# Gate inputs of the later groups as eight fp32 products in four column groups, placed between two groups; two steps of the sample tile moved by thirds of a block

## The chip, the cores and the metric

One NeuronCore of a Trainium2 chip runs the whole program. TensorE (PE, with its weight loads on PEld), VectorE (DVE), ScalarE (ACT), GpSimd (POOL) and the queue engine SyncE (SP) work side by side and wait for one another by semaphores. The metric is the device time of one execution in microseconds. Times below are medians of several executions, or, where a trace is read, those of one profiled execution.

## The reference, cut to what matters

One layer of a hybrid encoder trunk: 2048 prompt frames (16 tiles of 128 rows) and 8 running streams of 16 frames (one tile, number 16, called the sample tile).

```python
h = rmsnorm(x, norm_mix_pre)
P = h @ w_in                       # q|k|v (3*512) | z (512) | b (4) | a (4) | B | C | H
q, k, v = conv4 + SiLU, l2norm(q), l2norm(k)
beta = sigmoid(b_raw)              # one per row and head
g = -exp(a_log) * softplus(a_raw + dt_bias)
S_t = exp(g_t) (I - beta_t k_t k_t^T) S_{t-1} + beta_t k_t v_t^T      # chunked, 4 heads x 128 x 128
o = rmsnorm(S_t^T q_t) * SiLU(z)
x = x + rmsnorm(concat(o, B * conv3(C * H)) @ w_o)
x = x + rmsnorm((silu(h2 @ w_gate) * (h2 @ w_up)) @ w_down)
```

The change is in the gates `b` and `a`, which are eight columns of `w_in`, and in the recurrence of the sample tile, whose eight streams have a state of their own for each head.

## The kernel before

**Stages.** The first third of the time (to about 870 us of the trace) is the projection and the recurrence; then come the output projection, the feed-forward network and its down projection. The change is in the first stage alone.

**Groups and blocks.** The 17 row tiles are worked in five groups (`GROUPS`) of 4, 4, 3, 3 and 3 tiles; the sample tile is the last of group 3 (groups are counted from 0). For a group, `w_in` goes through PE as 28 blocks of 128 columns (`SEQS`). Each block is an fp32 product made of three fp32r products (high by high, high by low, low by high) for each of the eight slices `k` of the 1024 inputs: 24 matmuls at L317, with 512 or 384 moving columns. A block is issued in three thirds (slices 0 to 2, 3 to 5, 6 and 7); after each third the program runs the steps that stand in `events` for that moment. The moments of a group are numbered 0 to 83, three to a block, and what is due at 84 or later falls into the next group.

**What sets the order.** PE's order is written out by hand (`manual_schedule`); it is the order in which `plan` puts the steps, by the table `PLAN` and the constants in `plan`. The order of ACT, DVE, POOL and SP is made by a scheduler from priorities and a timing model. Every engine, and the SP queue, takes its instructions strictly in order.

**Rows of the next group.** While a group runs, the columns `xT` of the next one are loaded (`x_load`, L268), scaled in place by the rows' factors (`x_norm`, L274, DVE) and split into `hi` and `lo` (`split`, L231 on ACT and L232 on DVE) with the gain of the norm. The `hi` and `lo` pools have `KD + NHX` = 10 buffers, so two slices (`NHX`) are split ahead, and `next_rows` splits the other six at the group's end, as the last block frees the buffers. Loaded slices lie in a ring of `XKB` = 4 buffers, the last two in another.

**Gates.** `wba` holds the eight gate columns as high part (8) and rest (8). `gate_matmuls` (L469) multiplies them with `hi` and `lo` of all eight slices: 16 fp32r matmuls with 16 output rows. In groups 1 to 4 this is done at moment 2, after the first block. `gate_products` scales the result (L480, ACT), and `gate_rates` turns each tile (L487, from 16 rows to 128 x 16), adds the two halves on DVE (L493, L494) and goes on to the rates.

**Sample tile.** Its recurrence is spread over the end of group 3 and the start of group 4, head by head, 7 moments apart. For head h with u = 65 + 7h: load the states (u - 2 or u - 4), spread k and q over column groups on POOL (u), the products with the states (u + 3; L794, four column groups of 32, fp32), the solve (u + 5; L800), the output (u + 7; L804), and at u + 10 the update of the states: four products (L812) into four banks and eight DVE instructions (L814) that add them to the states. Then `out_norm` at u + 10 and `out_turn` (L708) at u + 15 of the last head.

**Banks.** PSUM's eight banks are shared: three `dbank` for blocks, two `tbank` for turning, two `gbank` and one `obank`. The update of a head takes both `gbank`, the `obank` and one `tbank`; the next user of each waits until DVE has read it. The chunks of the prompt tiles use the same banks: L727 and L743 (`gbank`), L735 (`obank`), then L749 (`gbank`), whose result DVE adds to the state at L752, and L757 (`obank`), read at L758; L708 (`tbank`), read at L710.

Of the kernel before, what the change touches and what calls it, by code (L numbers as in the profile page):

```python
# [17 lines left out]
P = 128  # L18
# [35 lines left out]
XKB = 4  # L54
NHX = 2
# [35 lines left out]
def kernel(  # L91
# [66 lines left out]
    with ExitStack() as ph:  # L158
# [313 lines left out]
        def gate_products(g, ps=None):  # L472
            n, c = g["n"], g["n"] * P
            ps = ps or gate_matmuls(g["hi"], g["lo"], n)
            bsb = xbuf()[:16]
            src = ps[:16, :c]
            if g["rb"] is not None:
                src = bsb[:, :c]
                V.tensor_mul(src, ps[:16, :c], g["rb"][:16, :c])
            A.activation(bsb[:, :c], src, AF.Identity, scale=gsct[:, 0:1], bias=gbia[:, 0:1])  # L480
            g["bsb"] = bsb

        def gate_rates(g):
            n, bsb = g["n"], g["bsb"]
            ps = bank()
            for i in range(n):
                T.transpose(ps[:, i * 16:(i + 1) * 16], bsb[:, i * P:(i + 1) * P], ident[:16, :16])  # L487
# [3 lines left out]
            ps3 = ps[:, :16 * n].rearrange("p (t c) -> p t c", c=16)  # L491
            y3 = yv[:, :m].rearrange("p (t c) -> p t c", c=8)
            V.tensor_copy(y3, ps3[:, :, 0:8])  # L493
            V.tensor_add(y3, y3, ps3[:, :, 8:16])  # L494
# [333 lines left out]
        def plan(g, nx, events):  # L828
# [8 lines left out]
            if gi:  # L837
                at(2, gate_products, g)
# [114 lines left out]
        gsct, gbia = vec[:16, 145:146], vec[:16, 146:147]  # L953
# [7 lines left out]
        wba = gp.tile([P, KD, 16], F32R, name="wba")  # L961
# [17 lines left out]
        rb2 = small.tile([P, W1], F32, tag="rb2", name="rb2", bufs=1)  # L979
# [13 lines left out]
        for gi, tiles in enumerate(GROUPS):  # L993
# [3 lines left out]
            if gi == 0:  # L997
                g["rb2"] = rb2
            nx = {} if gi + 1 < len(GROUPS) else None
# [643 lines left out]
def pack(i):  # L1643
# [22 lines left out]
    gates[:16, 4] = ([-1.0] * 4 + [1.0] * 4) * 2  # L1666
# [41 lines left out]
```

## Time and profile before

| | |
|---|---|
| median of 3 runs | 2463.88 us (2463.84 to 2475.24) |
| profiled execution | 2467.25 us, its span 2465.5 us |
| granted PE clock, mean of the span | 0.997 |
| PE busy | 2434.2 us, 99% of the span |
| DVE, ACT, POOL busy | 66%, 42%, 23% of the span |
| L317, the blocks of the first stage | 3360 matmuls |
| L469, the gates' products | 80 matmuls, 16 in each group |

The page gives busy times, the chain that ended last and groups of instructions. A row of the timeline gives the start in us, the length in us, the engine, the line, the operation with the tiles it writes and reads, and in brackets the idle time of the engine just before it and who ended that. A matmul on PE is longer than its share of the engine, since matmuls are pipelined: what one costs is read from one start to the next. An fp32 matmul appears as two instructions, an fp32r one as one.

### The profile page before, as it was taken

Reading aid. Unit: us, or ns where it says so; the run is one execution under the profiler, and the core shown is the slowest. Engines: PE = TensorE matmul, PEld = TensorE weight load, DVE = VectorE, ACT = ScalarE, POOL = GpSimd, SP = SyncE. Lnnn points to the kernel's source line nnn. Section 1 sums busy time; section 2 is a strip of 40 time slices with the busy share of each in tenths; the row PEclk is TensorE's granted clock in tenths of the full one; section 3 lists DMA queues with packets and bytes.
Section 4 is the critical chain, followed back from the end, with each engine's and each line's share of the span. In section 5 each row is a group of like instructions: output and inputs, shape, how many; then the busy total and the mean of one; then the engine's idle time right before and its main releaser. Section 6 shows DMA issues by size and latency. Waiting matters only on the chain.

```text
span 2465.5 us, 39355 instructions
## 1 busy us (share of the span) xinstructions
PE 2434.2 (99%) x14376; PEld 2227.0 (90%) x14376; DVE 1619.8 (66%) x3082; ACT 1045.3 (42%) x2338; POOL 578.9 (23%) x663
## 2 busy tenths in 40 slices
PE   9999999999999999999999999999999999999997
PEld 7888889999989988899999999999999988887886
DVE  6875755755666466888788744456456565677698
ACT  6545545546444343444343422234333345333343
POOL 1101001001110000146565300000000046455563
PEclk9999999999999999999999999999999999999999
DMA  7774655666776566598877788878988743333466
GB/s 273 262 243 155 223 194 195 248 225 225 261 257 226 182 204 226 188 335 298 293 267 258 279 258 269 256 241 275 305 295 284 249 147 117 115 113 124 131 222 192
DMA packets 263465, 561.38 MB, mean 228 GB/s; under 512 B 25188, under 2 KB 144680, under 8 KB 245992
## 3 DMA queue, kind: packets, MB, share of 16 engines
q1 hardware_dynamic: 146864, 486.98, 57.5%
q10 hardware_dynamic: 116184, 70.85, 9.5%
q8 instruction: 113, 1.85, 0.3%
q0 software_dynamic: 224, 1.05, 0.1%
q14 instruction: 80, 0.66, 0.1%
HBM read 400.09 MB, written 158.70 MB: 227 GB/s over the span
## 4 chain that ended last, share of the span: by engine, by line
PE 88%; DVE 5%; DMA 2%; issue 2%; POOL 2%; ACT 1%; SPq 0%; DVEq 0%; ACTq 0%; POOLq 0%
PE fbank L1335 35%; PE dbank L317 26%; PE fbank L1512 11%; PE dbank L1100 4%; PE tbank L1100 4%; DVE xr L1535 1%; PE tbank L375 1%; POOL dw L1185 1%; DVE acc L1472 1%; PE gbank L469 1%; PE gbank L580 1%; PE gbank L587 1%; PE obank L735 1%; PE gbank L727 1%; POOL as L1495 1%
## 5 line engine op out<-in xcount | busy, mean ns | idle before, releaser
L1335 PE MATMUL fbank<-xh,fw 128*128 128x384 f32 (+1 forms) x3696 | 897.7, 326 | 2.5 <-ACT m L1369 2.3
L317 PE MATMUL dbank<-hi,w 128*128 128x384 f32 (+1 forms) x2240 | 655.1, 363 | 1.3 <-ACT w L296 0.7
L1335 PEld LDWEIGHTS fbank<-xh,fw 128*128 128x128 f32 x3696 | 651.1, 188 | 3.7 <-ACT m L1369 2.6
L1335 PE MATMUL fbank<-xl,fw 128*128 128x384 f32 (+1 forms) x1848 | 601.8, 326 | 0.0
L317 PEld LDWEIGHTS dbank<-hi,w 128*128 128x128 f32 x2240 | 413.6, 188 | 39.4 <-DVE w L297 1.3
L1512 PE MATMUL fbank<-dw,as 128*128 128x512 f32 x1782 | 420.1, 392 | 3.0 <-DVE as L1495 0.9
L1512 PEld LDWEIGHTS fbank<-dw,as 128*128 128x128 f32 x1782 | 332.9, 188 | 81.7 <-POOL as L1495 3.5
L317 PE MATMUL dbank<-lo,w 128*128 128x384 f32 (+1 forms) x1120 | 400.5, 358 | 0.5 <-DVE lo L232 0.5
L1335 PEld LDWEIGHTS fbank<-xl,fw 128*128 128x128 f32 x1848 | 346.9, 188 | 0.0
L317 PEld LDWEIGHTS dbank<-lo,w 128*128 128x128 f32 x1120 | 211.2, 189 | 16.8 <-DVE lo L232 0.8
L1495 POOL TENSOR_TENSOR as<-ar,as 128x256 fp32r<-128x256 f32 (+1 forms) x202 | 184.5, 925 | 170.7 <-ACT as L1492 162.9
L1472 DVE TENSOR_TENSOR acc<-acc,fbank 128x512 f32<-128x512 f32 x248 | 164.9, 681 | 90.1 <-PE fbank L1512 77.0
L1185 POOL TENSOR_TENSOR dw<-dr,dw 128x512 fp32r<-128x512 f32 x48 | 70.5, 1481 | 496.3 <-ACT dw L1183 496.2
L1492 ACT CAST as<-ar 128x256 fp32r<-128x256 f32 (+1 forms) x287 | 116.4, 427 | 166.5 <-PE fbank L1512 128.8
L1310 ACT CAST fw<-rg 128x512 fp32r<-128x512 f32 x124 | 77.2, 622 | 229.9 <-PE fbank L1335 132.6
L321 DVE SCALAR_TENSOR_TENSOR acc<-R,vec,acc 128x512 f32<-128x512 f32 (+2 forms) x180 | 120.9, 672 | 33.2 <-ACT acc L358 28.2
L1383 DVE TENSOR_TENSOR c<-u,fbank 128x384 f32<-128x384 f32 (+1 forms) x66 | 34.8, 528 | 96.5 <-PE fbank L1335 96.5
L1379 DVE TENSOR_TENSOR m<-m,m 128x384 f32<-128x384 f32 (+1 forms) x44 | 23.1, 525 | 83.0 <-ACT m L1369 82.9
L1311 POOL TENSOR_TENSOR fw<-rg,fw 128x512 fp32r<-128x512 f32 x44 | 65.3, 1484 | 44.6 <-ACT fw L1310 44.3
L1386 ACT ACTIVATE c<-c 128x384 f32<-128x384 f32 (+1 forms) x66 | 33.4, 506 | 93.6 <-DVE c L1385 93.6
L350 POOL COPY hist<-R 128x3 f32<-128x3 f32 x60 | 20.3, 338 | 220.8 <-ACT R L326 171.4
L1381 ACT ACTIVATE m<-fbank 128x384 f32<-128x384 f32 (+1 forms) x66 | 31.2, 473 | 92.2 <-PE fbank L1335 76.6
(386 smaller groups left out, 3590.7 us busy)
## 6 DMA issues: line engine op xcount, KB each, us to landing
w<-wsplit SPq DMA_DIRECT2D x105, 1024.0 KB, 4.9
fw<-fsplit SPq DMA_DIRECT2D x188, 512.0 KB, 4.7
fsplit<-fw SPq DMA_DIRECT2D x94, 512.0 KB, 3.7
partd<-pt ACTq DMA_DIRECT2D x86, 384.0 KB, 6.2
rg<-in_w_gu SPq DMA_DIRECT2D x62, 512.0 KB, 4.2
wsplit<-w SPq DMA_DIRECT2D x28, 1024.0 KB, 4.8
wr<-in_w_in SPq DMA_DIRECT2D x34, 512.0 KB, 5.9
ar<-partd SPq DMA_DIRECT2D x43, 384.0 KB, 3.1
```

The costliest lines, as they stand in the source:

```text
L317: T.matmul(ps[:, :c], l[:, k, :], r[k][:, :c], start=(k == 0 and r is hi and l is wh), stop=(k == KD - 1 and l is wl))
L321: r = V.scalar_tensor_tensor(acc, raw(d), w[:, d:d + 1], acc, op0=ALU.mult, op1=ALU.add)
L1100: T.matmul(pss[n], m_[:, j, :], w_[k][:, n * 512:(n + 1) * 512], start=(k == 0 and ci == 0), stop=(k == KD - 1 and ci == 2))
L1185: e.tensor_tensor(out=w[1], in0=v, in1=w[0].bitcast(F32), op=ALU.subtract)
L1310: A.copy(w[:, 0], v)
L1311: e.tensor_tensor(out=w[:, 1], in0=v, in1=w[:, 0].bitcast(F32), op=ALU.subtract)
L1335: T.matmul(ps, w_[:, c], b_[k][:, :hw], start=(first and k == 0 and ci == 0), stop=(k == KH - 1 and ci == 2), skip_group_check=not first)
L1383: V.tensor_add(c21, u2, b3)
L1472: return eng.tensor_tensor(out=dst, in0=dst, in1=ps, op=ALU.add)
L1492: ins = A.copy(a[:, 0, :n], v)
L1495: e.tensor_tensor(out=a[:, 1, :n], in0=v, in1=a[:, 0, :n].bitcast(F32), op=ALU.subtract)
L1512: T.matmul(ps, a[:, x_, q * P:(q + 1) * P], w[y_], start=(start and q == 0 and ci == 0), stop=(q == c - 1 and ci == 2), skip_group_check=True)
```

## The change

Gates of groups 1 to 4. A new function `gate_parts` is called at the head of `next_rows`, so on PE between the last block of a group and the first of the next. It multiplies the unsplit, scaled slices with `wbag`, the gate columns times the gain of the norm, padded to 32 columns: eight fp32 products, slice `k` in column group `k % 4` and so in PSUM partitions `32 * (k % 4)` and up, two rounds adding to one another. One ACT instruction moves all 128 partitions to `bsb`. `gate_rates` turns 128 x 128 a tile, and one DVE reduction adds the four column groups. Group 0 keeps the old way. The 16 fp32r products at moment 2 go.

Rows. `NHX` goes from 2 to 1 (9 buffers, so one slice is split ahead and seven behind) and `XKB` from 4 to 6. `wba` and `rb2` move to shared buffers that are idle then.

Sample tile. For heads 0, 2 and 3 the update of the states comes at u + 9, one third of a block earlier; for head 1 it stays at u + 10. `out_turn` comes at u + 17, two thirds later.

```diff
-XKB = 4
-NHX = 2
+XKB = 6
+NHX = 1
...
+        def gate_parts(nx, n):
+            c = n * P
+            ps = bank()
+            for e in range(2):
+                for q in range(4):
+                    k = 4 * e + q
+                    T.matmul(ps[32 * q:32 * q + 32, :c], wbag[:, k, :], nx["xk"][k][:, :c], start=not e, stop=bool(e))
+            bsb = cp.tile([P, W1], F32, tag="vraw", name="bsb", bufs=NKV)
+            A.activation(bsb[:, :c], ps[:, :c], AF.Identity, scale=gsct[:, 0:1], bias=gbia[:, 0:1])
+            nx["bsb"] = bsb
...
+            w = 16 if g["rb"] is not None else P
             for i in range(n):
-                T.transpose(ps[:, i * 16:(i + 1) * 16], bsb[:, i * P:(i + 1) * P], ident[:16, :16])
+                T.transpose(ps[:, i * w:(i + 1) * w], bsb[:, i * P:(i + 1) * P], ident[:w, :w])
...
+            else:
+                V.tensor_reduce(out=y3, in_=ps[:, :P * n].rearrange("p (t q c) -> p t c q", q=4, c=32)[:, :, 0:8], axis=AX.X, op=ALU.add)
...
-            if gi:
-                at(2, gate_products, g)
...
-                    thread((u - (2 if h else 4), u, u + 3, u + 5, u + 7, u + 10), sample_head(g, npr, h))
+                    thread((u - (2 if h else 4), u, u + 3, u + 5, u + 7, u + (10 if h == 1 else 9)), sample_head(g, npr, h))
                 at(u + 10, lambda: out_norm(g, npr, smp["o"]))
-                at(u + 15, lambda: out_turn(g, npr, smp["o"]))
+                at(u + 17, lambda: out_turn(g, npr, smp["o"]))
...
         def next_rows(gi, nx):
             tiles = GROUPS[gi]
+            gate_parts(nx, len(tiles))
             for k in range(NHX, KD):
                 x_split(tiles, k, nx)
...
+        wbag = gp.tile([P, KD, 32], F32, name="wbag")
+        G.memset(wbag, 0.0)
...
+            V.tensor_mul(wbag[:, :, 0:8], wba_r, g_pre.unsqueeze(2).broadcast_to([P, KD, 8]))
```

Line numbers shift in the changed file: the sample tile's products with the states are L794 before and L806 after, its update L812 and L824 (DVE: L814 and L826), the turning L708 and L720, a chunk's L749, L757, L752 and L758 become L761, L769, L764 and L770.

The gates on PE in group 4, before: they follow the output of head 2 (L804), after the group's first block (the fp32r products go on in pairs to 16).

```order
L317 MATMUL dbank<-lo,w_7513 128x384
L317 MATMUL dbank<-hi,w_7513 128x384
L804 MATMUL gbank<-qT,dt 128x128
L469 MATMUL gbank<-hi,wba 16x384
L469 MATMUL gbank<-lo,wba 16x384
L469 MATMUL gbank<-hi,wba 16x384
```

The same gates on PE after, between the last block of group 3 (w_7377) and the first of group 4 (w_7485):

```order
L317 MATMUL dbank<-lo,w_7377 128x384
L317 MATMUL dbank<-hi,w_7377 128x384 x2
L317 MATMUL dbank<-lo,w_7377 128x384
L317 MATMUL dbank<-hi,w_7377 128x384
L478 MATMUL gbank<-xk,wbag 32x384 x6
L478 MATMUL gbank<-xt,wbag 32x384 x2
L317 MATMUL dbank<-hi,w_7485 128x384
```

Eight products stand there now instead of sixteen, and they read `xk` and `xt`, not `hi` and `lo`.

The update of head 0 on PE, before: it stands nine block products (one third) after the chunk's L708, L749 and L757, and directly ahead of the products of head 1.

```order
L317 MATMUL dbank<-hi,w_7219 128x384 x2
L317 MATMUL dbank<-lo,w_7219 128x384
L317 MATMUL dbank<-hi,w_7219 128x384
L812 MATMUL gbank<-dt,AU 128x256 x2
L812 MATMUL obank<-dt,AU 128x256
L812 MATMUL tbank<-dt,AU 128x256
L794 MATMUL gbank<-st,kz 32x128 x8
```

The update of head 0 on PE, after (L824 is the update; L720, L761 and L769 are the chunk's turning, its state product and its output product):

```order
L317 MATMUL dbank<-hi,w_7152 128x384
L824 MATMUL gbank<-dt,AU 128x256 x2
L824 MATMUL obank<-dt,AU 128x256
L824 MATMUL tbank<-dt,AU 128x256
L720 MATMUL tbank<-cst,o 128x128 x4
L761 MATMUL gbank<-yt,kl 128x128 x4
L769 MATMUL obank<-yt,dt 128x128 x4
L317 MATMUL dbank<-hi,w_7195 128x384
```

The update moved ahead of the three steps of the chunk, which use the same banks.

DVE at the same place, before (xk and xt are the rows of the next group, yo an output of a block, ot the turned chunk, S the chunk's state, st the states of the sample tile):

```order
L455 TENSOR_TENSOR yo<-acc,dbank 128x256
L457 TENSOR_TENSOR yo<-acc,dbank 128x128
L274 TENSOR_TENSOR xt<-xt,rb 128x384
L710 SCALAR_TENSOR_TENSOR ot<-tbank,vec,sz 128x512
L274 TENSOR_TENSOR xt<-xt,rb 128x384
L752 SCALAR_TENSOR_TENSOR S<-S,eL,gbank 128x128 x4
L758 TENSOR_TENSOR o<-o,obank 128x512
L814 SCALAR_TENSOR_TENSOR st<-st,eLs,gbank 128x128 x4
L814 SCALAR_TENSOR_TENSOR st<-st,eLs,obank 128x128 x2
```

DVE at the same place, after:

```order
L455 TENSOR_TENSOR yo<-acc,dbank 128x256
L457 TENSOR_TENSOR yo<-acc,dbank 128x128
L274 TENSOR_TENSOR xt<-xt,rb 128x384
L826 SCALAR_TENSOR_TENSOR st<-st,eLs,gbank 128x128 x2
L274 TENSOR_TENSOR xt<-xt,rb 128x384
L826 SCALAR_TENSOR_TENSOR st<-st,eLs,gbank 128x128 x2
L826 SCALAR_TENSOR_TENSOR st<-st,eLs,obank 128x128 x2
L826 SCALAR_TENSOR_TENSOR st<-st,eLs,tbank 128x128 x2
L722 SCALAR_TENSOR_TENSOR ot<-tbank,vec,sz 128x512
L764 SCALAR_TENSOR_TENSOR S<-S,eL,gbank 128x128 x4
L770 TENSOR_TENSOR o<-o,obank 128x512
```

The eight updates of the states moved ahead of the chunk's turning, state and output, and still stand behind the block output and one scaling of rows.

More of the change, by code (lines that the diff above doesn't have):

```diff
@@ L470, in gate_matmuls, with gate_products @@
             return ps
-        def gate_products(g, ps=None):
+        def gate_parts(nx, n):
[8 more added lines that the diff above has]
+            nx["bsb"] = bsb
+        def gate_products(g, ps):
             n, c = g["n"], g["n"] * P
-            ps = ps or gate_matmuls(g["hi"], g["lo"], n)
             bsb = xbuf()[:16]
[L476 to L480, printed above, removed]
+            src = bsb[:, :c]
+            V.tensor_mul(src, ps[:16, :c], g["rb"][:16, :c])
+            A.activation(bsb[:, :c], src, AF.Identity, scale=gsct[:16, 0:1], bias=gbia[:16, 0:1])
             g["bsb"] = bsb
@@ L960 @@
         nega = gp.tile([P, 4], F32, name="nega")
-        wba = gp.tile([P, KD, 16], F32R, name="wba")
+        wba = wk.tile([P, 256], F32, tag="pr", name="wba").bitcast(F32R)[:, :16 * KD].rearrange("p (k c) -> p k c", c=16)
+        wbag = gp.tile([P, KD, 32], F32, name="wbag")
+        G.memset(wbag, 0.0)
         with tc.issue_after(mark["hi"].ins):
@@ L978 @@
         matmuls(firsts[2], pending[2][1:], hi, lo, c, range(6, KD))
-        rb2 = small.tile([P, W1], F32, tag="rb2", name="rb2", bufs=1)
+        rb2 = wk.tile([P, NS, P], F32, tag="st", name="rb2", bufs=2).rearrange("p s v -> p (s v)")[:, :W1]
         G.memset(U, 0.0)
@@ L998 @@
                 g["rb2"] = rb2
+            else:
+                g["bsb"] = nx["bsb"]
             nx = {} if gi + 1 < len(GROUPS) else None
@@ L1665, in pack @@
     gates[:, 0:4] = f["a_log"].reshape(1, 4)
-    gates[:16, 4] = ([-1.0] * 4 + [1.0] * 4) * 2
+    gates[:, 4] = ([-1.0] * 4 + [1.0] * 4) * 16
     gates[4:8, 5] = f["dt_bias"].reshape(4)
```

9 lines of the change are left out of this document (5 added, 4 removed).

## The prediction

> **What bounds the kernel now.** I read the page first: busy shares, then the chain of work that ended last.
>
> ```profile
> PE 2434.2 (99%) x14376; PEld 2227.0 (90%) x14376; DVE 1619.8 (66%) x3082; ACT 1045.3 (42%) x2338; POOL 578.9 (23%) x663
> PE 88%; DVE 5%; DMA 2%; issue 2%; POOL 2%; ACT 1%; SPq 0%; DVEq 0%; ACTq 0%; POOLq 0%
> ```
>
> PE is busy 99% of the span and makes 88% of the chain. So the time is PE's work plus PE's few waits, and the change is worth what it takes from either. Work on ACT, DVE, POOL or SP counts only where PE then waits. I therefore cost every part in starts on PE, from one instruction to the next, and make the sum against the profiled execution of 2467.25 us; the median of the runs is 2463.88 us, 3.4 us lower, and I carry the difference over to it.
>
> **Gates, removed.** The windows of L469 in groups 1 to 4, each from its first product to the next instruction of PE:
>
> ```profile
> 202.70:206.39 3.69, 3.69 (x16) 1.42 (x15) 1.00 0.67 213
> 405.91:408.78 2.87, 2.87 (x16) 1.48 (x16) 1.00 0.89 291
> 560.83:563.63 2.80, 2.80 (x16) 1.42 (x15) 1.00 0.76 233
> 714.21:717.08 2.87, 2.87 (x16) 1.48 (x16) 1.00 1.08 352
> sum 12.23, PE 12.23 PEld 5.80; mean PE 3.06 PEld 1.45
> ```
>
> All 12.23 us are PE's and go.
>
> **Gates, added.** Eight fp32 products in four column groups, 512 or 384 columns. The nearest row has the same form with 128 columns: L794 in the sample tile, sixteen products (32 instructions), four column groups, each with moving data of its own.
>
> ```profile
> 673.39 0.34 PE L317 MATMUL dbank<-hi,w 128*128 128x384 f32 x1
> 673.66 0.64 PE L794 MATMUL gbank<-st,kz 128*32 128x128 f32 x16
> 674.67 0.38 PE L749 MATMUL gbank<-yt,kl 128*128 128x128 f32 x1
> ```
>
> Sixteen products take 674.67 - 673.66 = 1.01 us. Entering costs 673.66 - 673.39 = 0.27 us where the 384-column products otherwise start 0.17 us apart (2.80 us by 16, above), so 0.10 us for the change of form. By columns, eight products of 384 are 8 x 3 / 16 x 1.01 = 1.52 us, of 512 2.02 us. Four groups: 2.02 + 3 x 1.52 = 6.6 us. With 0.1 us for going in and as much for coming out, 4 x 0.2, it is 7.4 us. The 1.01 us holds a fixed tail that doesn't grow with the columns, so I take 7.0. The upper end is eight products one after the other, priced by full-width fp32:
>
> ```profile
> 194.08 1.05 PE L743 MATMUL gbank<-r,U 128*128 128x128 f32 x8
> 194.89 0.48 PE L317 MATMUL dbank<-hi,w 128*128 128x512 f32 x1
> ```
>
> Four products in 0.81 us are 0.20 us for 128 columns; 8 x 4 x 0.20 + 3 x 8 x 3 x 0.20 = 20.9 us, with the switches 21.7. L794's sixteen would then take 3.2 us; they take 1.01, in the same form, so I stay at 7.0. **Gain 5.2 us** (between 5.6 and a loss of 9.5).
>
> The weights are a question of their own, because each product loads 32 columns of them.
>
> ```profile
> L794 PEld LDWEIGHTS gbank<-st,kz x64: 106/109/110, 673.7 to 723.5; 128*32 128x32 f32 x64
> 707.46 0.41 PEld L794 LDWEIGHTS gbank<-st,kz 128*32 128x32 f32 x16 [1.60 <-issue]
> ```
>
> Sixteen loads of 109 ns fit into 0.41 us, so they overlap one another and the running products. The Trainium skill, TensorE: Matmul & The Clock Gate, section The mechanism (of row and column tiling), says that a load overlaps running matmuls only when the row groups differ; here all products use all rows, so by that rule it would not. The trace disagrees with the rule and decides; what the rule would cost stands with the rivals.
>
> No wait is added for the gates' inputs: the scaled slices are ready long before, since the splits made from them run during the last block. `NHX` 1 leaves one split more on ACT and DVE behind; it is hidden by the gate products, which now run ahead of the first block, and shows at each boundary if they don't. The eviction of the gates goes to ACT behind the splits, and PE needs nothing of it until `gate_rates`. `XKB` 6 lets SP issue two row loads of group 0 earlier, ahead of one store and one weight load of its queue; three weight buffers cover that: nothing.
>
> **Rates.** Turning goes from 16 rows to 128.
>
> ```profile
> 728.56 0.34 PE L317 MATMUL dbank<-hi,w 128*128 128x384 f32 x1
> 728.83 0.35 PE L487 MATMUL gbank<-cst,xk 16*128 16x16 f32 x3
> 729.12 0.45 PE L317 MATMUL dbank<-hi,w 128*128 128x384 f32 x1
> ...
> 423.00 0.60 PE L708 MATMUL tbank<-cst,o 128*128 128x128 f32 x4
> 423.36 0.42 PE L317 MATMUL dbank<-hi,w 128*128 128x384 f32 x1
> ```
>
> Three small ones take 0.29 us and 0.10 us to enter; four full ones take 0.36 us, so three 0.27. **Gain 0.1 us a group, 0.5 in all.**
>
> **A wait in group 3 that is filled.** The turning of the last chunk of group 2 waits for ACT at the start of group 3:
>
> ```profile
> 557.75 0.34 PE L317 MATMUL dbank<-hi,w 128*128 128x384 f32 x1
> 558.28 1.28 ACT L703 ACTIVATE o<-o,ofr 128x128 f32<-128x128 f32 x4 [2.67 <-POOL ofr L147]
> 558.74 1.21 PE L708 MATMUL tbank<-cst,o 128*128 128x128 f32 x4 [0.64 <-ACT o L703]
> 559.70 0.42 PE L317 MATMUL dbank<-hi,w 128*128 128x384 f32 x1
> ```
>
> From 557.93 (one start after 557.75) to 559.70 are 1.77 us for work of 0.36: 1.4 us of wait. The chain through POOL and ACT doesn't depend on the gates, and PE comes 1.6 us later, with the gate products done meanwhile. The eviction that ACT does ahead of L703 ends before 558.28. **Gain 1.3 us** (0 to 1.4).
>
> **Head 2.** Its update moves one third ahead of head 3's products.
>
> ```profile
> 721.36 0.48 PE L812 MATMUL gbank<-dt,AU 32*128 32x256 f32 x2
> 722.09 1.12 DVE L814 SCALAR_TENSOR_TENSOR st<-st,eLs,gbank 128x128 f32<-128x128 f32 x4 [4.83 <-PE tbank L812]
> 723.23 0.64 PE L794 MATMUL gbank<-st,kz 128*32 128x128 f32 x16 [1.16 <-DVE st L814]
> ...
> 735.27 0.48 PE L812 MATMUL gbank<-dt,AU 32*128 32x256 f32 x2
> 735.91 0.44 PE L317 MATMUL dbank<-hi,w 128*128 128x384 f32 x1
> ```
>
> An update costs PE 0.64 us (735.27 to 735.91); here PE stood until 723.23. Six block products of 0.17 now fill 1.0 of that wait, less 0.1 for a switch more. **Gain 0.9 us.** Head 1's update stays, and with it the same wait. Head 3's has block products behind it before and after: nothing.
>
> **Head 0: what is late next.** Its update moves ahead of a chunk's L708, L749 and L757, which need the same banks.
>
> ```profile
> 688.04 0.60 PE L708 MATMUL tbank<-cst,o 128*128 128x128 f32 x4
> 691.95 0.86 PE L812 MATMUL gbank<-dt,AU 32*128 32x256 f32 x4
> 694.56 0.44 PE L317 MATMUL dbank<-hi,w 128*128 128x384 f32 x1
> ...
> 688.35 0.56 DVE L274 TENSOR_TENSOR xk<-xk,rb 128x384 f32<-128x384 f32 x1 [0.82 <-DMA xk<-in_xT]
> 689.35 0.55 DVE L274 TENSOR_TENSOR xt<-xt,rb 128x384 f32<-128x384 f32 x1
> ```
>
> Today PE needs 6.5 us from 688.04 to 694.56. Without waits the new order needs 0.64 (update), 0.4 and 0.9 (L708, L749), 0.8 (L757), 1.8 (nine block products with switches) and 1.0 (L794), 5.6 us. But DVE stands behind a load until 688.35, and the eight state updates come after L455, L457 and this L274, so not before 689.82. Two of them free a `gbank` about 690.6 (0.28 us each, by 1.12 for four, and a little for the semaphore); PE wants it for L749 at 689.1: 1.5 us. The `obank` for L757 comes after the second L274 (0.5 us) and four more, about 692.2, where PE is ready at 691.6: 0.6 us. So 7.7 us: **loss 1.2 us** (from a gain of 0.9 to a loss of 1.6).
>
> **Turning of the sample tile.** Today it asks for a third `tbank` where there are two.
>
> ```profile
> 743.92 0.82 PE L375 MATMUL tbank<-cst,kT 128*128 128x128 f32 x6
> 747.19 0.47 ACT L400 COPY kt<-tbank 128x384 f32<-128x384 f32 x1
> 747.71 0.66 PE L708 MATMUL tbank<-cst,sz 128*128 128x128 f32 x4 [2.98 <-ACT kt L400]
> ```
>
> L375's six take 0.65 us (six of 0.11), so L708 was due at 744.57 and came at 747.71: 3.1 us. Two thirds later means 18 block products, 18 x 0.174 = 3.1 us, in between, and ACT frees the bank at 747.66, as PE arrives. Its store and the SP load behind it are late by nothing against today. **Gain 3.1 us** (2 to 3.1).
>
> And a second part, seen in the granted clock of the windows around it (the number behind the five engines):
>
> ```profile
> 744.00:749.00 5.00, 2.02 (x16) 1.76 (x15) 2.91 (x6) 4.28 (x8) 0.38 (x2) 1.00 0.87 287
> 749.00:752.40 3.40, 3.40 (x13) 3.40 (x12) 1.36 (x6) 0.00 (x0) 2.27 (x1) 0.50 0.55 166
> ```
>
> Right behind the wait the clock is 0.50 for 3.4 us, worth 1.7 us of full-speed work. Without the wait I count it gone. **Gain 1.7 us** (0 to 1.7). The Trainium skill, TensorE: Matmul & The Clock Gate, section What's actually happening, puts the halving down to a free-running window of about 3.4 us with too little work. The trace agrees in length; by that rule the phase decides whether an execution has this stretch, and one without it gains only the other terms.
>
> **Sum.** 5.2 + 0.5 + 1.3 + 0.9 - 1.2 + 3.1 + 1.7 = 11.5 us: the profiled execution at 2455.8, the median at 2452.4, or 2454.1 where the runs before had no half clock to lose. I forecast 2453 us, 0.44% faster, so inside the 0.5% (12.3 us) that a measurement of this kernel can about tell from no change. Its own range is 2451 to 2456.
>
> **Rivals.**
> - Head 0 costs nothing: the banks come free in time, and 1.2 lost become 0.9 gained. 2450.9 us, just faster than the bound. For it: head 0 also waits today. Against it: DVE's order and the load that holds it until 688.35.
> - Head 0's wait halves the clock for 3.4 us, as the turning's did: 2454.7 us. For it: 2.1 us of waiting among small work. Against it: 1.16 us at head 2 did nothing.
> - The column groups don't run side by side with long rows: gates cost 21.7 instead of 7.0. 2467.7 us, slower than before by 0.15%. It decides the sign when the gates cost over 18 us, so with fewer than 1.2 products at once. Against it: L794.
> - Weight loads don't overlap products: 16 loads of 0.11 us at four boundaries add 7 us, 2460 us. This is what the rule on row groups gives. Against it: sixteen loads in 0.41 us.
>
> **How the numbers follow.** Forecast 0.58; head 0 free 0.18; half clock at head 0 0.10; groups one after the other 0.06; loads in line 0.03; 0.05 for a wait that I don't see, past 0.5% slower. Range: from 2449.5 (head 0 free, the gates at 6.6 and the half clock gone from every run, 2449.9) to 2460, loads in line. Faster by over 0.5%: head 0 free, and 0.06 of the forecast's upper edge: 0.24. Slower: 0.05. The rest, 0.71, is within.
>
> **What would show it.** In the trace after: L478 at four boundaries with about 2.0, 1.5, 1.5 and 1.5 us to the next start; no wait at the turning in group 3; L806 of head 3 starting within 0.2 us of its turn; L761 and L769 waiting for DVE's L826 for 1.5 and 0.6 us; no wait at the sample's L720 and no clock of 0.50 behind it. The prediction is wrong if L478 takes over 3 us anywhere, if a first block after a boundary waits for `hi` or `lo`, or if head 0 shows no wait.

## The result, and the profile after

| | before | after |
|---|---|---|
| median of 11 runs each | 2468.55 us (2463.84 to 2477.11) | 2456.28 us (2454.60 to 2459.01) |
| ratio after/before, 95% interval | | 0.9953 [0.9944, 0.9962] |
| profiled execution, its span | 2467.25, 2465.5 us | 2459.01, 2457.2 us |
| first product of the output projection | 870.50 us | 860.93 us |

So the change brings 0.47%, within the 0.5%, at 2456.28 us where 2453 was forecast; that is 0.3 us past the forecast's own range of 2451 to 2456, and inside the wider one. The three runs of before that the forecast started from had a median of 2463.88 us; with eight more it is 2468.55. As a ratio the sum of the prediction (11.5 of 2467.25 us) was 0.9953; that this is the measured one to the last digit is in part luck, as the part on why the prediction was right says.

The page of the changed kernel, busy shares and chain: PE sets the time as before.

```profile
PE 2428.1 (99%) x14376; PEld 2222.2 (90%) x14376; DVE 1619.9 (66%) x3079; ACT 1045.7 (43%) x2338; POOL 578.6 (24%) x664
PE 87%; DVE 6%; DMA 2%; issue 2%; POOL 2%; ACT 1%; SPq 0%; DVEq 0%; ACTq 0%; POOLq 0%
```

**Where the time went.** L317 does the same 3360 matmuls in the same order in both kernels, so the start of each block can be set beside its twin. All in us from the start of the span:

| first product of | before | after | difference |
|---|---|---|---|
| group 1, second block | 206.38 | 204.57 | -1.81 |
| group 2, second block | 408.77 | 405.69 | -3.08 |
| group 3, second block | 563.63 | 557.92 | -5.71 |
| group 3, 27th block (behind head 0) | 697.43 | 692.69 | -4.74 |
| group 4, second block | 717.08 | 711.10 | -5.98 |
| group 4, 6th block (behind heads 2 and 3) | 739.67 | 733.23 | -6.44 |
| group 4, 8th block (behind the turning) | 754.08 | 742.86 | -11.22 |
| group 4, 10th block | 762.40 | 752.75 | -9.65 |
| output projection | 870.50 | 860.93 | -9.57 |
| end of the span | 2465.5 | 2457.2 | -8.3 |

Read matmul by matmul, the steps of that difference sort into the prediction's terms: gates -5.14 (-1.63, -1.17, -1.17, -1.17), the wait of group 3 -1.33, rates -0.49, head 0 +1.15, head 2 -0.38, turning and half clock -4.78, and one that no term foresaw, +1.57 between the 8th and the 10th block of group 4. Another -0.17 is there before group 1 begins, so it is not the gates'. They add up to -9.57.

The gates in the timeline of PE, at the start of groups 1 and 4:

```profile
194.89 1.48 PE L478 MATMUL gbank<-xk,wbag 128*32 128x512 f32 x10
...
196.75 0.50 PE L317 MATMUL dbank<-hi,w 128*128 128x512 f32 x1
...
705.03 1.16 PE L478 MATMUL gbank<-xk,wbag 128*32 128x384 f32 x10
...
706.46 0.44 PE L317 MATMUL dbank<-hi,w 128*128 128x384 f32 x1
```

From the first gate product to the next block are 1.86 us with 512 columns and 1.43 with 384.

Head 0 on PE (and in the third row the wait behind head 1's update, which was not moved), then on DVE:

```profile
682.91 0.66 PE L720 MATMUL tbank<-cst,o 128*128 128x128 f32 x4
684.68 1.13 PE L761 MATMUL gbank<-yt,kl 128*128 128x128 f32 x8 [1.11 <-DVE st L826]
686.18 1.13 PE L769 MATMUL obank<-yt,dt 128*128 128x128 f32 x8 [0.37 <-DVE st L826]
702.75 0.49 PE L806 MATMUL gbank<-st,kz 128*32 128x128 f32 x9 [1.22 <-DVE st L826]
...
682.46 0.56 DVE L274 TENSOR_TENSOR xk<-xk,rb 128x384 f32<-128x384 f32 x1 [0.80 <-DMA xk<-in_xT]
683.93 0.60 DVE L826 SCALAR_TENSOR_TENSOR st<-st,eLs,gbank 128x128 f32<-128x128 f32 x2
684.92 0.59 DVE L826 SCALAR_TENSOR_TENSOR st<-st,eLs,gbank 128x128 f32<-128x128 f32 x2
```

PE waits twice for DVE's state updates. DVE itself stands behind a load until 682.46, and the first two updates come at 683.93, behind a block's output and a scaling of rows.

The turning of the sample tile: no wait ahead of it any more.

```profile
741.20 0.34 PE L317 MATMUL dbank<-hi,w 128*128 128x384 f32 x1
741.37 0.60 PE L720 MATMUL tbank<-cst,sz 128*128 128x128 f32 x4
741.73 0.42 PE L317 MATMUL dbank<-hi,w 128*128 128x384 f32 x1
```

Two waits that the prediction did not have. The products of head 3 wait for the load of their states, and a block of group 4 waits for its weights (SP rows are the issues of the loads):

```profile
712.86 0.38 SPq L793 DMA_DIRECT2D st<-in_state  x1
716.93 0.64 PE L806 MATMUL gbank<-st,kz 128*32 128x128 f32 x16 [0.56 <-DMA st<-in_state]
...
742.51 0.32 SPq L563 DMA_DIRECT2D dt<-grow  x1
743.57 0.55 SPq L909 DMA_DIRECT2D sz<-mixs  x1
744.22 0.61 SPq L287 DMA_DIRECT2D w<-wsplit  x1
752.75 0.41 PE L317 MATMUL dbank<-hi,w 128*128 128x384 f32 x1 [1.40 <-DMA w<-wsplit]
```

The load of `sz` can go only when the turning has freed its tile, and SP takes its loads in order, so the weights behind it went out at 744.22. They took 8.4 us to land; the weight load of before that stands alone there takes 5.9.

Behind the output projection 1.3 us of the gain are lost again. The windows of the feed-forward network (the number behind the five engines is the granted clock):

```profile
1395.27:1398.68 3.41, 1.31 (x8) 0.98 (x6) 3.41 (x8) 0.67 (x2) 0.00 (x0) 1.00 0.77 223
1398.68:1402.09 3.41, 3.02 (x9) 3.03 (x10) 3.33 (x7) 1.23 (x3) 0.00 (x0) 0.50 0.22 84
```

PE works for 1.31 of 3.41 us, and then has half its clock for 3.41 us. Before had a like wait there (2.31 us at 1408.45) without the half clock.

### The profile page after: what moved, and what is told of

It is laid out like the page before. It is cut to its first block, busy times and chain, and to the rows that moved or that the text cites. A ratio compares the mean times of both kernels' runs of the same rounds, so it can differ in the third digit from the quotient of the medians.

```text
span 2457.2 us, 39354 instructions
## 1 busy us (share of the span) xinstructions
PE 2428.1 (99%) x14376; PEld 2222.2 (90%) x14376; DVE 1619.9 (66%) x3079; ACT 1045.7 (43%) x2338; POOL 578.6 (24%) x664
## 3 DMA queue, kind: packets, MB, share of 16 engines
q0 software_dynamic: 224, 1.05, 0.1%
## 4 chain that ended last, share of the span: by engine, by line
PE 87%; DVE 6%; DMA 2%; issue 2%; POOL 2%; ACT 1%; SPq 0%; DVEq 0%; ACTq 0%; POOLq 0%
PE fbank L1351 36%; PE dbank L317 26%; PE fbank L1528 11%; PE dbank L1116 4%; PE tbank L1116 4%; POOL dw L1201 1%; DVE xr L1551 1%; PE tbank L375 1%; DVE acc L1488 1%; PE gbank L592 1%; PE gbank L599 1%; PE obank L769 1%; POOL as L1511 1%; PE obank L747 1%; PE gbank L739 1%
## 5 line engine op out<-in xcount | busy, mean ns | idle before, releaser
L317 PE MATMUL dbank<-hi,w 128*128 128x384 f32 (+1 forms) x2240 | 655.6, 363 | 2.2 <-DMA w<-wsplit 1.4
L317 PEld LDWEIGHTS dbank<-hi,w 128*128 128x128 f32 x2240 | 412.6, 188 | 43.9 <-issue 4.0
L317 PE MATMUL dbank<-lo,w 128*128 128x384 f32 (+1 forms) x1120 | 399.6, 357 | 0.3 <-DVE lo L232 0.3
L317 PEld LDWEIGHTS dbank<-lo,w 128*128 128x128 f32 x1120 | 210.7, 188 | 16.6 <-DVE lo L232 0.6
```

The source lines that it names most:

```text
L317: T.matmul(ps[:, :c], l[:, k, :], r[k][:, :c], start=(k == 0 and r is hi and l is wh), stop=(k == KD - 1 and l is wl))
```

## The experiments

Single runs of one kernel differ by several us, so most comparisons go by the first product of the output projection (OP), which ends the stage that the change is in. The start of the program alone moves it: in the eleven profiles of changed kernels with four column groups the second block of group 1 comes at 204.39 to 204.97 us, ahead of what most of the edits touch. So a difference of a few tenths at OP is read only where single waits or steps show it. "Held" is the idle time of DVE ahead of L1422 (L1406 in the numbering of before). All kernels:

| run | OP at, us | from there to the end | DVE held by L1422 | PE's wait near 1396 | profiled time |
|---|---|---|---|---|---|
| before | 870.50 | 1594.97 | 7.15 | 2.31 | 2467.25 |
| after | 860.93 | 1596.31 | 7.40 | 2.49, half clock | 2459.01 |
| after_again | 861.04 | 1592.86 | 5.21 | 0.37 | 2455.67 |
| gates_alone | 864.61 | 1594.73 | 5.99 | 1.15 | 2461.12 |
| moves_alone | 868.32 | 1593.60 | 5.25 | 0.41 | 2463.76 |
| one_group | 878.32 | 1593.54 | 5.28 | 0.43 | 2473.63 |
| pairs | 863.78 | 1593.12 | 5.18 | 0.33 | 2458.70 |
| head0_back | 859.12 | 1592.01 | 5.03 | 0.28 | 2452.90 |
| sz_late | 860.11 | 1592.12 | 5.25 | 0.40 | 2454.00 |
| dt_sz_late | 859.49 | 1598.70 | 7.41 | 2.51, half clock | 2459.97 |
| u8 | 858.06 | 1600.02 | 9.54 | 1.90 and 2.48, half clock | 2459.85 |
| pt_late | 860.51 | 1595.66 | none | under 0.25 | 2457.95 |
| best | 856.63 | 1599.32 | 10.34 | 2.69 and 1.03, half clock | 2457.73 |
| best_pt | 856.32 | 1595.37 | none | 1.53 | 2453.46 |

### The two halves of the change apart

gates_alone is the changed kernel with the sample tile's steps where they were:

```diff
-thread((u - (2 if h else 4), u, u + 3, u + 5, u + 7, u + (10 if h == 1 else 9)), sample_head(g, npr, h))
+thread((u - (2 if h else 4), u, u + 3, u + 5, u + 7, u + 10), sample_head(g, npr, h))
...
-at(u + 17, lambda: out_turn(g, npr, smp["o"]))
+at(u + 15, lambda: out_turn(g, npr, smp["o"]))
```

> The changed kernel with the sample tile's steps where they were before (all updates at u + 10, the turning at u + 15). Measured by the first product of the output projection, which stands at 870.50 us before and at 860.93 in the changed kernel. Theory (the parts add up): the gates with the wait of group 3 bring 6.6 us (by the block starts of the two traces), so 870.5 - 6.6 - 0.3 = 863.6 us at the output projection, less if no window behind the turning's wait is at half clock; the sample's turning waits 3.1 us again. Rival (the gates moved the turning's wait too, so that the moves earned nothing of their own): 861 us and no wait at the turning.

moves_alone is the kernel before with the opposite edit.

> The kernel before with the moves of the sample tile alone. Theory (parts add up): head 2 gains 0.4 to 0.8 us, head 0 loses 1.0, the turning's wait of 3.1 us goes and the half clock behind it (1.7), and the weight load waits 1.4 us as in the changed kernel, since on SP the load of sz stands ahead of it here too: 870.5 - 3 = 867.5 us at the output projection, with waits of 1.1 and 0.4 us at head 0. Rival (the weight load is late only because the gates shortened the blocks ahead): no wait for the weights, 866 us.

Measured: OP at 864.61 and 868.32, where 863.6 and 867.5 were expected. The gates alone bring 5.89 us, with one wait that no other run has at this place:

```profile
651.47 0.65 PE L694 MATMUL gbank<-AU 64*64 64x64 f32 x8 [1.16 <-DVE AU L673]
```

This execution is 0.23 us behind that of before when group 1 begins. Counted from there, and without the step of 1.19 us at this wait, the gates bring 7.3 us; 0.28 of them stand at head 2, whose wait is 0.88 us here instead of 1.16. The other 7.0 are what the terms give (5.14 + 1.33 + 0.49 = 6.96). The sample's turning has its wait again (2.98 us idle) and a clock of 0.50 behind it.

The moves alone bring 2.18 us: turning and half clock 4.75, less 1.05 at head 0, 0.13 at head 2 and 1.38 at the weights. At head 2 a gain of 0.4 to 0.8 had been expected; the products of head 3 wait 1.07 us for the load of their states. The weights are late in the kernel before too once the turning moves:

```profile
760.12 0.41 PE L317 MATMUL dbank<-hi,w 128*128 128x384 f32 x1 [1.23 <-DMA w<-wsplit]
```

Together the two bring 8.07 of the 9.57 us, and 1.16 of the rest is the wait at 651.47, whose cause stays open. So the parts add up to within a few tenths, and the weight wait comes from the turning's move, not from the gates: moves_alone has it, gates_alone doesn't.

### Do the column groups run side by side?

one_group puts all eight products of a group into one column group (32 rows are turned then, and a copy takes the place of the reduction):

```diff
-T.matmul(ps[32 * q:32 * q + 32, :c], wbag[:, k, :], nx["xk"][k][:, :c], start=not e, stop=bool(e))
+T.matmul(ps[0:32, :c], wbag[:, k, :], nx["xk"][k][:, :c], start=not k, stop=k == KD - 1)
...
```

> The changed kernel with the eight gate products of a group in one column group, adding to one another in 32 partitions; 32 rows are turned instead of 128, one DVE copy takes the place of the reduction. Theory (in four column groups they run four at a time): eight products one after the other take 8 x 3 x 0.20 = 4.8 us with 384 columns and 6.4 us with 512 instead of 1.43 and 1.85 measured, so 15 us more in all, and the output projection starts at 875 to 876 us. Rival (products of 32 columns are cheap by themselves, the column groups have little to do with it): 1.5 to 2 us a group as now, 861 us.

OP came at 878.32, 17.4 us later. The timeline at group 1:

```profile
195.34 5.34 PE L478 MATMUL gbank<-xk,wbag 128*32 128x512 f32 x12
200.52 1.88 PE L478 MATMUL gbank<-xt,wbag 128*32 128x512 f32 x4
202.33 0.50 PE L317 MATMUL dbank<-hi,w 128*128 128x512 f32 x1
```

6.99 us instead of 1.86; with 384 columns 5.28 instead of 1.43, where 6.4 and 4.8 had been expected. That is 3.7 times, so four products at once and a short tail; the rival falls.

pairs keeps four column groups, but issues 0, 0, 1, 1, 2, 2, 3, 3 instead of 0, 1, 2, 3, 0, 1, 2, 3:

```diff
-for q in range(4):
-    k = 4 * e + q
+for q, f in ((2 * e, 0), (2 * e, 1), (2 * e + 1, 0), (2 * e + 1, 1)):
+    k = 4 * f + q
...
```

> The changed kernel with the two products of each column group next to one another (groups 0, 0, 1, 1, 2, 2, 3, 3 instead of 0, 1, 2, 3, 0, 1, 2, 3). Theory (PE starts strictly in order, and a product for a busy column group holds all behind it): five steps of 0.6 us instead of two for 384 columns, 3.0 us instead of 1.43, and 4.0 instead of 1.85 for 512; the output projection starts 7 us later, at 868 us. Rival (each column group takes its own products whatever the order): 1.43 us as now, 860.9 us.

```profile
705.37 1.17 PE L478 MATMUL gbank<-xk,wbag 128*32 128x384 f32 x10
...
706.81 0.44 PE L317 MATMUL dbank<-hi,w 128*128 128x384 f32 x1
```

1.44 us, no more than in the changed kernel: my theory fell, the rival holds. Matmul by matmul, four of the sixteen instructions start within 0.04 us of one another, the next four 0.35 us in, the third four 0.67. In one_group, where all share a column group, each starts 0.32 us or more behind the one before. So four that start together belong to four column groups, and the second product of a group, which stands ahead of the first of the next group in the program, starts with the third four. (OP is late at 863.78 for another reason: the weights came 2.5 us late in this run, with a clock of 0.50 behind. Why they came that late is not known.)

### Head 0, head 1 and head 2

head0_back undoes the move of head 0 alone:

```diff
-u + (10 if h == 1 else 9)
+u + (9 if h > 1 else 10)
```

> The changed kernel with head 0's update back at u + 10; heads 2 and 3 stay at u + 9. Theory (head 0's move lost, since PE then waits for DVE at the state product and the output product of a chunk): the two waits of 1.11 and 0.37 us go, the old ones of 0.3 and 0.5 us come back, and the output projection starts 1.0 us earlier than in the changed kernel, at 859.9. Rival (head 0's move is free, the waits only moved): 860.9, no difference.

OP at 859.12, 1.81 us earlier. From the second block of group 3 to the first of group 4 it takes 147.39 us instead of 148.54, so 1.15 us are head 0's, where 1.0 was expected; 0.4 more stand at head 3's products, whose wait for the load of their states shrinks from 0.56 to 0.19, and the rest is the start of the program. In place of the two waits stands one short one, at the products of head 1:

```profile
687.50 0.64 PE L806 MATMUL gbank<-st,kz 128*32 128x128 f32 x16 [0.19 <-PE tbank L824]
```

u8 goes the other way and updates heads 0 and 1 still earlier:

```diff
-u + (10 if h == 1 else 9)
+u + (9 if h > 1 else 8)
```

> The changed kernel with the updates of heads 0 and 1 at u + 8, so one third earlier for head 0 and two for head 1. Theory (PE's waits there are the 2.5 to 3 us that DVE needs behind an update, and work put between fills them): head 1's wait of 1.6 us falls under 0.5; head 0's two waits (1.11 and 0.37) shrink to about 1.0 together, since DVE is still held by the load of xk; the output projection starts 1.5 to 2 us earlier than in the changed kernel, at 859.0 to 859.4. Rival (the turning at u + 9 of head 1 now meets busy banks): the wait only moves there, 860.9.

OP at 858.06, 2.87 us earlier, more than expected. The rows of L761 and L769 at head 0, of L806 at head 1, and of L806 at head 3:

```profile
683.66 1.06 PE L761 MATMUL gbank<-yt,kl 128*128 128x128 f32 x8
684.87 1.13 PE L769 MATMUL obank<-yt,dt 128*128 128x128 f32 x8 [0.16 <-DVE st L826]
...
700.34 0.43 PE L806 MATMUL gbank<-st,kz 128*32 128x128 f32 x8
...
713.87 0.64 PE L806 MATMUL gbank<-st,kz 128*32 128x128 f32 x16
```

Of the waits of 1.11 and 0.37 (head 0), 1.22 (head 1) and 0.56 us (head 3's products) 0.16 is left. The last also shows where that wait came from: the states of head 3 are loaded into the tile that head 1's store frees (in the changed kernel the store lands at 712.79 and the load goes out at 712.86), and head 1 was late.

### The weight wait: the queue or the transfer?

sz_late ties the load of `sz` behind a much later weight load; PE, DVE and ACT keep their order.

```diff
-nc.sync.dma_start(out=sz, in_=mixs[gi][:, :, i * P:(i + 1) * P])
+with tc.issue_after(wloads[-1].ins): nc.sync.dma_start(out=sz, in_=mixs[gi][:, :, i * P:(i + 1) * P])
```

> The changed kernel with the load of sz tied behind a much later weight load; the order of every engine but SP is the same. In the changed kernel a block waits 1.40 us for its weights at 752.75, whose load went out at 744.22, behind the load of sz, which SP issued at 743.57. Theory A (the queue: SP stood behind sz, whose tile is free only after the turning): the load goes out at 742.9 as its buffer comes free, the wait falls to 0 to 0.2 us, the output projection starts at 859.4 to 859.6. Theory B (the transfer: 768 KB of dt and two weight loads share the DMA engines, whenever the load goes out): the load still lands past 752, the wait stays over 0.8 us, 860.3 to 860.9.

```profile
742.43 0.32 SPq L563 DMA_DIRECT2D dt<-grow  x1
742.90 0.33 SPq L287 DMA_DIRECT2D w<-wsplit  x1
...
751.93 0.41 PE L317 MATMUL dbank<-hi,w 128*128 128x384 f32 x1 [0.74 <-DMA w<-wsplit]
```

The load goes out at 742.90, 1.3 us earlier, and the wait falls from 1.40 to 0.74: about half by the queue (A), half left, so neither theory alone. (In the eight runs that have the turning late and leave SP's order as it is, this wait is 1.23 to 2.52 us, so the halves are rough.) dt_sz_late also puts the load of `dt` behind that weight load: `gate_decay` hands the load out instead of issuing it, and in group 4 it is issued a block later, tied (`behind`) to the last weight load:

```diff
-at(decay, gate_decay, g)
+dl = []; at(decay, lambda: dl.extend(gate_decay(g)))
+at(decay + (3 if gi == 4 else 0), lambda: behind(dl[0]) if gi == 4 else dl[0]())
```

> The kernel of the run sz_late with the load of dt (768 KB) moved behind the weight load that PE waits for; PE's order is the same. In sz_late that load went out at 742.90, 1.3 us earlier than in the changed kernel, and PE still waited 0.74 us. Theory (the transfer ahead of it on the queue, dt, takes the DMA engines it needs): the load lands in about 6 us, as the weight loads do that stand alone (5.9), and the wait is gone; the output projection starts 0.7 us earlier than in sz_late, at 859.4 us, if DVE doesn't then wait for dt. Rival (the weight load is slowed by the next one, issued 4.2 us behind it): the wait stays over 0.5 us.

```profile
743.22 0.32 SPq L287 DMA_DIRECT2D w<-wsplit  x1
743.63 0.38 SPq L563 DMA_DIRECT2D dt<-grow  x1
```

The load lands in 5.1 us and PE doesn't wait; OP at 859.49 as expected. So the other half was the transfer of `dt` (768 KB) ahead of it. The two kernels below that hold this edit, best and best_pt, have no such wait either.

### What happens behind the output projection

The table shows 1592 to 1600 us for the same work. PE's wait near 1396 follows one instruction of DVE, L1422, which the scheduler has put early and which must wait until a store of `pt` has left the tile. The changed kernel once more:

> The changed kernel once more, to tell what in its first profile belongs to the kernel and what to that execution. Theory (the hold of DVE by L1422 and the clock of 0.50 at 1398 us are of the execution: sz_late and pairs, with the same order on DVE, had holds of 5.2 us instead of 7.4): the output projection starts at 860.5 to 861.2 us again, with the waits of 1.1 and 0.4 us at head 0, 1.4 (1.0 to 2.5) for the weights, but the hold, PE's wait near 1396 and the time behind come out another way: with a hold of about 5.2 us a wait under 0.5, no clock of 0.50 there and 1592 to 1593 us from the output projection on, so a run at 2454 to 2455 us. Rival (they belong to the kernel): hold 7.4, wait 2.5, 0.50 behind it, 1596 us. Median 2455 to 2458 us, ratio to before 0.9945 to 0.996.

L1422 and the waiting matmul, first in the profile of the changed kernel, then in its repetition:

```profile
1381.58 0.56 DVE L1422 TENSOR_TENSOR pt<-a,a 128x384 f32<-128x384 f32 x1 [7.40 <-DMA fw<-fsplit]
1399.07 0.69 PE L1351 MATMUL fbank<-xh,fw 128*128 128x384 f32 x1 [2.49 <-ACT m L1385]
```

```profile
1379.82 0.56 DVE L1422 TENSOR_TENSOR pt<-a,a 128x384 f32<-128x384 f32 x1 [5.21 <-DMA partd<-pt]
1397.32 0.44 PE L1351 MATMUL fbank<-xh,fw 128*128 128x384 f32 x1 [0.37 <-ACT m L1385]
```

(In the first row the wait is put down to another load; the tile that L1422 writes is `pt`.) The same kernel, OP 0.1 us apart, with a hold of 5.21 instead of 7.40, 0.37 instead of 2.49 us of wait, full clock, and 3.45 us less in the end: what the first profile lost there belongs to the execution. The store that ends the hold went out at 1364.61 and landed at 1381.46 in the first, at 1365.22 and 1379.70 in the second. Its five runs had a median of 2458.05 us (2454.50 to 2460.68; 2455 to 2458 had been expected), 0.9957 [0.9943, 0.9970] of before.

pt_late lets L1422 go only behind L1415:

```diff
-V.tensor_sub(pt[:, 1, :hw], a11, a21)
+with tc.issue_after(gmark["V"].ins): V.tensor_sub(pt[:, 1, :hw], a11, a21)
```

> The changed kernel with DVE's L1422 (feed-forward) tied behind L1415 of its own block; PE's order is the same, the recurrence isn't touched. In the ten profiles so far the time from the first product of the output projection to the end of the span lies between 1592.0 and 1600.0 us for the same work, and follows one wait: L1422 holds DVE for 5.0 to 9.5 us, until a store of the tile pt has landed, and behind it PE stands 0.3 to 4.4 us near 1396. Theory (that hold is the cause, and the changed kernel's profile drew a long one): L1422 no longer holds DVE, PE's wait near 1396 falls to 0.4 us or less, no clock of 0.50 behind it, 1591 to 1592.2 us from the output projection on, and a median of 2453.5 to 2454.5 us, 2 us under the changed kernel's 2456.3. Rival (DVE waits for the same store one instruction later, at L1414 or L1415): the wait stays, 1593 to 1598 us, and the median is that of the changed kernel.

The hold at L1422 and the wait near 1396 went, as expected. The time did not follow: 1595.66 us from OP on, and a median of 2457.95 us, 0.9951 [0.9939, 0.9964] of before, as the changed kernel. Against head0_back's profile it loses 1.0 us at another wait for ACT (0.65 at 1351.58), 0.9 at the start of the down projection and some 1.8 in steps of 0.3 to 0.7 through it. The edit also changed the order of SP, ACT and POOL in the feed-forward network, so whether those are its price or the execution's stays open. Nor did the store let go of DVE altogether: ACT issues the next store from its own queue (L1388), and that issue waits for the same landing. ACT stands 2.43 us there until 1381.92, and DVE 2.67 us until 1382.47 for the cast that follows on ACT.

best has dt_sz_late and u8 together, best_pt has pt_late as well.

> The changed kernel with the loads of sz and dt late (the run dt_sz_late) and the updates of heads 0 and 1 at u + 8 (the run u8). Theory (the two add up: the weight wait of 1.7 us in u8 goes, the waits of heads 0 and 1 stay gone): the output projection starts at 856.0 to 856.6 us, 4.5 us earlier than in the changed kernel; with 1592 to 1600 us behind it a time of 2450 to 2458 us, median near 2452, ratio to before 0.993 to 0.995. Rival (the earlier blocks meet the next late load): a weight wait of over 0.5 us comes back at another block, 857 us or later.

> Both together. Theory: the output projection at 856.0 to 856.6, 1591 to 1592.2 us behind it, time 2448.8 to 2450.6 us with little spread, ratio to before 0.992 to 0.9935. Rival (what is gained ahead is given back in the feed-forward network, because its weights come no earlier): the span from the output projection on grows by what was gained, 2453 us or more.

OP came at 856.63 and 856.32, 4.3 and 4.6 us ahead of the changed kernel: the two repairs add up. best gave it back:

```profile
1381.84 0.56 DVE L1422 TENSOR_TENSOR pt<-a,a 128x384 f32<-128x384 f32 x1 [10.34 <-DMA fw<-fsplit]
1394.45 0.69 PE L1351 MATMUL fbank<-xh,fw 128*128 128x384 f32 x1 [2.69 <-ACT m L1383]
1399.31 0.45 PE L1351 MATMUL fbank<-xh,fw 128*128 128x384 f32 x1 [1.03 <-ACT m L1385]
```

A hold of 10.34 us, two waits and a half clock: median 2456.68 us, 0.9946 [0.9933, 0.9958], no better than the changed kernel. best_pt has no hold and ran at 2451.97 us (2451.57 to 2453.46), 0.9929 [0.9915, 0.9942], beside the same runs of before: the fastest of all, ahead of both kernels. It is 1.4 us over what was expected: PE still waits 1.53 us at 1394.29, though nothing holds L1422. The same store holds DVE by way of ACT instead, the first row being ACT's issue of the next store:

```profile
1380.07 0.37 ACTq L1388 DMA_DIRECT2D partd<-a  x1
1380.48 0.51 ACT L1274 CAST xh<-fh 128x384 fp32r<-128x384 f32 x1 [5.87 <-DMA partd<-pt]
1381.02 0.56 DVE L1275 TENSOR_TENSOR xl<-fh,xh 128x384 fp32r<-128x384 f32 x1 [6.10 <-ACT xh L1274]
```

So pt_late takes away one of two instructions that wait for this landing (1380.05 here). That PE's wait at 1394 follows from the other fits these rows; no run takes that second wait away, so it is not shown. Whether earlier arrival itself lengthens the hold (9.5 and 10.3 us in u8 and best, the two earliest kernels without pt_late, but 5.0 in head0_back, 1.1 us behind u8) is not settled.

## Why the prediction was right, and where it was not

- **Gates.** 7.0 us for the new products: 1.86 + 3 x 1.43 = 6.2 us measured, with about 0.2 at each boundary for going in and coming out 7.1. Gain 5.2 forecast, 5.14 found. The row that carried it, sixteen products of L794 in 1.01 us, held for long rows too, and one_group shows that its reason was right.
- **Weight loads.** L478 loads 32 columns 64 times at 106 to 110 ns, all inside those 6.2 us, so they overlap. By the rule of the Trainium skill, TensorE: Matmul & The Clock Gate, section The mechanism, that loads overlap only across row groups, they would have cost 7 us more; the trace disagrees again. (The same section also lets a load go ahead when it targets the background weight buffer.) The page of before spoke against that rival too: there PEld is busy 90% of the span beside PE's 99%.
- **Rates, group 3.** 0.5 and 1.3 us forecast, 0.49 and 1.33 found.
- **Head 0.** Waits of 1.5 and 0.6 us forecast from DVE's order, counted by when the next start was due. So counted they are 1.33 and 0.61 (due 0.44 us behind L720 at 682.91 and 0.89 behind L761 at 684.68, the steps of before); the 1.11 and 0.37 in the rows are PE's idle time alone. Loss 1.2 forecast, 1.15 found, 1.15 by undoing it.
- **Head 2.** 0.9 us forecast, 0.38 found. The step "six block products of 0.17 now fill 1.0 of that wait" looked at DVE alone. What is late next is the load of head 3's states: 0.56 us here, 1.07 us in moves_alone, gone in u8. The trace of before held the sign: that load went out at 717.62 and landed at 723.09, 0.14 us before PE went on at 723.23. DVE ended at 723.21, 0.12 us later than the load, and the bracket of a row names only the last.
- **Turning.** 3.1 and 1.7 us forecast, 4.78 found together.
- **The step that failed** is the sentence behind it: "Its store and the SP load behind it are late by nothing against today." SP's order had the load of `sz` ahead of a weight load, with `dt` in front of both, and PE has no spare time there: 1.57 us lost, about half by the queue, half by the transfer.
- **The half clock.** The execution profiled after had a stretch of its own at 1398.68, so its span shows 8.3 us where OP shows 9.57; the repetition had none, and its span of 2453.9 us is 11.6 under that of before. The prediction had said that the phase decides; it had not seen that another wait, 650 us later, could bring a half clock.

The mechanism is shown up to OP: of 11.5 us forecast 9.57 are found there, and the two misses, 0.5 and 1.6 us, make the difference up to a few tenths. The ratio of 0.9953 is luck in its last digits: by OP it would be 0.9961, by the spans of the two profiled executions 0.9966, and the medians are 12.27 us apart. Where the medians' part beyond OP's 9.57 comes from stays open: what follows OP takes 1592 to 1600 us in the profiles, and there is one profile of before. The rivals fell one by one: head 0 was not free, no clock of 0.50 followed it, products and loads did not run in line.

## What to carry to other kernels

When a step moves later, look at what its tile frees: a load that waits for that tile holds everything behind it on its queue, and a weight load with 8.3 us between free buffer and need (742.86 to 751.18) had no room for 1.3 us in the queue and 768 KB in front. Among several things that end a wait, the trace names the last; look how close behind the next one stands before counting the whole wait as a gain. A wait of PE behind DVE can be filled from the other side: moving the update earlier, with block products between it and the next user of its banks, took out nearly all the waits that a third of a block had only shifted. And gains of a few us must be read at a fixed place of the program, since the end moved by 3.5 us between two executions of the same kernel, beside one store that took 16.9 us to land in the first and 14.5 in the second.

## What was not expected of the hardware

**The clock.** In each trace the changes of the granted clock inside the span lie whole multiples of 3.4133 us after its first record (before: 744.106 us, 218 times; after: 1392.638 us, 408 times). Within that grid, PE's idle time in one window decides about the next. Three windows in a row of u8, then two of before:

```profile
1393.83:1397.24 3.41, 1.74 (x10) 1.75 (x11) 3.41 (x7) 1.61 (x4) 1.72 (x1) 1.00 0.49 154
1397.24:1400.66 3.42, 0.94 (x6) 0.62 (x5) 3.39 (x8) 1.36 (x3) 0.00 (x0) 1.00 0.47 140
1400.66:1404.07 3.41, 3.41 (x12) 3.41 (x11) 3.24 (x7) 0.54 (x2) 0.00 (x0) 0.50 0.21 69
```

```profile
1404.36:1407.77 3.41, 1.79 (x11) 1.47 (x9) 3.41 (x9) 0.53 (x1) 0.00 (x0) 1.00 0.65 185
1407.77:1411.19 3.42, 2.73 (x14) 2.48 (x15) 3.35 (x8) 1.38 (x3) 0.00 (x0) 1.00 0.31 122
```

1.67 us idle left the next window at 1.00, 2.48 halved it; before's wait of 2.31 us fell across two windows, 1.62 in the first, and did nothing. Over the 14 profiles, the first window and the last 30 us of each span apart, all 7 windows with 2.10 to 2.51 us idle were followed by 0.50 and none of the 45 with 1.0 to 1.67. In those last 30 us, where PE runs out of work, one with 1.94 was followed by 0.50 (dt_sz_late) and one with 1.74 was not (best), so the border lies near there. The Trainium skill, TensorE: Matmul & The Clock Gate, section What's actually happening, gives the free-running window of 3413 ns, and the traces agree with it to the digit; its table asks for an idle window, where 1.9 to 2.1 of 3.4 us were enough here.

**Order on PE.** In pairs, matmuls of other column groups start ahead of one that stands before them in the program and waits for its own column group. The changed kernel shows it by the tiles' names: the program has all products with `xk` ahead of the two with `xt`, and one_group starts them so (twelve instructions, then four), but here two on `xt` start ahead of the last two on `xk`:

```profile
195.79 0.60 PE L478 MATMUL gbank<-xt,wbag 128*32 128x512 f32 x2
196.21 0.60 PE L478 MATMUL gbank<-xk,wbag 128*32 128x512 f32 x2
```

So that every engine takes its instructions strictly in order, as the part on the kernel before has it, is not so for the starts of PE's products in different column groups. The same page, section The mechanism, says that matmuls keep the program's order in start and end; the trace disagrees for the starts.
